# Half A's FFN in half B's order, four weight-sum jobs elsewhere, and the conditioning weights through the second merge

## The chip, the cores and the metric

One core of a Trainium2 chip runs the whole layer in one launch. The metric is device time in microseconds (us): the median of the runs, and beside it one execution with a hardware profile. The engines are named as in the profile: PE (TensorE), DVE (VectorE), ACT (ScalarE), POOL (GpSimd) and SP (SyncE, which here only issues DMAs).

## The reference

A layer for 1024 prompt tokens and 8 x 4 sample tokens, which share weights. The parts around the change:

```python
mod = silu(c) @ ada_w + ada_b                 # conditioning: shifts, scales, gates per sequence
sh1, sc1, gt1, sh2, sc2, gt2 = split(mod, 6)
u = (rmsnorm(x, g1) * (1 + sc1) + sh1) @ w_in # u_x, u_g, u_q, u_k, u_v, u_r, u_lr, u_ga, u_gb
h_lru = rg_lru(causal_conv(u_x)); y_a = h_lru * gelu(u_g)
y_b = rmsnorm(gla(u_q, u_k, u_v, ...)) * silu(u_r)
m = sigmoid(u_ga) * (y_a @ proj_a) + sigmoid(u_gb) * (y_b @ proj_b)
x = x + gt1 * (m @ w_out)
h2 = rmsnorm(x, g2) * (1 + sc2) + sh2
f1, f2 = split(h2 @ ffn_w1, 2)                # d_model 1024, d_ff 2816
x = x + gt2 * ((silu(f1) * f2) @ ffn_w2)
```

All is float32, and the last columns of `mod` (scale and gate of the FFN) are not needed before the second norm.

## The kernel before

**Halves.** The tokens are worked in two halves, one after the other: A has N = 512 prompt tokens, B has 544 (512 prompt tokens and the 32 sample tokens). Activations lie transposed, channels on partitions in tiles of 128 and tokens along the columns. D is 8 tiles, the FFN's inner width 22 tiles (f0 to f21), the recurrence's 10.

**Products.** Each float32 operand is split into a high and a low part of type fp32r; a product is three matmuls (lines L452, L453, L454). A weight comes by an SP DMA into a buffer of the pool "raw" (5 buffers, `load_raw`, L145), is split by ACT (L154, high part) and DVE (L155, the rest) into a buffer of the pool "hl" (3 buffers), and is used at the full width of 512 columns, or in A's output projection and first FFN tiles in two pieces of 256 columns.

**The fast form.** `products` (L1421, L1429 to L1431) computes a 2 x 2 block product with 7 block products in place of 8. It works on half the columns (256 in A), and needs sums of weight blocks and of activation blocks. Weight sums are made on the chip and kept in device memory: by `weight_sums` (tiles `s1<f>`, `s2<f>`: two SP loads of 512 KB into "raw", four DVE steps L352 to L355, two POOL stores L356 and L357 into `wsum<f>`; one job for each f, taken one at a time with `next(sums_of)`), and by `paced_sums` (the pool "sums", POOL loads L388, DVE L392 to L396, POOL stores L398). A tile f in the fast form is 84 matmuls for both weight halves; the second product of six k tiles in the fast form (`ffn2_fast`) is 252 in place of 144 of full width. For the latter, `keep` stores the block sums of the activations instead of the tiles.

**The FFN of A before.** `back`: after the output projection (`out_proj` on columns 0 to 255, then 256 to 511), f0 to f3 in two column pieces (`ffn1_first`), f4 and f5 whole (`ffn1`), f6 to f10 fast, then the second product over k tiles 0 to 10 directly (`ffn2(0, 11)`, out `f3psa`), with four sum jobs at its output tiles j = 0, 2, 4, 6; then f11 to f21 fast, and `ffn2(11, 22)`. B does f0 to f3, `ffn2(0, 4)`, f4 to f10 fast, `ffn2_fast(0)` over k tiles 4 to 9, and so on.

**Conditioning.** `ada_w` comes in 12 column chunks cc of four 512 KB loads (`ada<cc><k>`, L203, into an S buffer), each used by a group of small matmuls (`adaps<cc>`, L212; eight records in the profile), and closed by a transpose (`adat`, L223). `s.ada(1)` gives out one step. Chunks 0 to 9 are done earlier; what is left, cc 10 and 11 for the most part, was drained just before the merge of A. The merge (`merge_a`) has eight steps j: 24 matmuls for the gate (`gapsa<j>`), 30 for the projection (`papsa<j>`, weights `pa0a<j>` and `pa1a<j>`). Before it, `merge_b` does the same for the other branch (`pbpsa<j>`), with the last pair of recurrence tiles (`lma8`, `laa9`, `yaa8`, `yaa9`) between.

**What sets the order.** A tile scheduler orders the instructions of each engine by its own estimates and by the pools: S (17 large buffers), X (8), T (6). Each engine works its list strictly in order; SP's list is the order of the loads, and a load that waits for a buffer holds all behind it.

Of the kernel before, what the change touches and what calls it, by code (L numbers as in the profile page):

```python
# [27 lines left out]
LEVELS = (64, 32, 16, 8, 4, 2, 1)  # L28
EPS = 1e-6
EARLY = 4  # L30
FAST = (6, 4)
KF = (3, 2, 1, 0, 4, 6, 8, 5, 7, 9, 10, 12, 14, 11, 13, 15, 16, 17, 18, 19, 20, 21)
KORD = (0, 2, 4, 6, 1, 3, 5, 7)
GATES = KD // 2
# [20 lines left out]
def hybrid_layer(ctx, tc, I, O):  # L55
# [25 lines left out]
    tp = ctx.enter_context(tc.tile_pool(name="tp", bufs=6))  # L81
    axp = ctx.enter_context(tc.tile_pool(name="axp", bufs=2, space=PSUM))
    drp = ctx.enter_context(tc.tile_pool(name="drp", bufs=1, space=bass.MemoryType.DRAM))
    wsum = {f: drp.tile([P, 2048], F32, name=f"wsum{f}") for f in range(FAST[1], NF)}
    wsumg = [drp.tile([P, 2048], F32, name=f"wsumg{c}") for c in range(GATES)]
    wsum2 = {(q, g): drp.tile([P, 1536], F32, name=f"wsumf{q}{g}") for q in range(4) for g in range(2)}

# [259 lines left out]

    def weight_sums():

        for f in range(FAST[0], NF):  # L350
            r1, r2 = load_raw(I["ffn1"][2 * f], 1024, f"s1{f}"), load_raw(I["ffn1"][2 * f + 1], 1024, f"s2{f}")
            dve.tensor_add(r2[:, 512:1024], r2[:, 0:512], r2[:, 512:1024])  # L352
# [9 lines left out]
    def paced_sums():  # L362

        jobs = []
        halves = lambda t, u, c: t.rearrange("p (n u) -> p n u", n=2)[:, :, c * u:(c + 1) * u]
        def columns(sums, src):
            for c in range(2):
                to = [halves(sums[:, v * 1024:(v + 1) * 1024], 256, c) for v in range(2)]
                jobs.append((256, [halves(t, 256, c) for t in src], to))

        def rows(g):
            for q in range(4):
                c = P * (4 + 6 * g)
                to = [halves(wsum2[q, g][:, v * 768:(v + 1) * 768], 384, 0) for v in range(2)]
                jobs.append((384, [halves(I["ffn2"][2 * q + v][:, c:c + 768], 384, 0) for v in range(2)], to))

        for f in range(FAST[1], FAST[0]):
            columns(wsum[f], [I["ffn1"][2 * f + v] for v in range(2)])
        rows(0)
        for c in range(GATES):  # L380
            columns(wsumg[c], [I["w_in"][T_GA + 2 * c + v] for v in range(2)])
        rows(1)
        for k, (u, src, to) in enumerate(jobs):
            r = [wp.tile([P, 768], F32, tag="sums", name=f"sums{k}{v}", bufs=2) for v in range(2)]
            rv = [t[:, :2 * u].rearrange("p (n u) -> p n u", n=2) for t in r]
            for v in range(2):
                pool.tensor_copy(r[v][:, 0:1], pace[0][:, 0:1])
                pool.dma_start(rv[v], src[v])  # L388
            yield 1
            r1, r2 = rv  # L390
            last = len(traced())
            dve.tensor_add(r2[:, 1], r2[:, 0], r2[:, 1])  # L392
            behind(last)
            dve.tensor_sub(r2[:, 0], r1[:, 0], r2[:, 0])
            dve.tensor_sub(r1[:, 0], r2[:, 1], r1[:, 0])
            dve.tensor_sub(r1[:, 1], r1[:, 1], r1[:, 0])  # L396
            for v in range(2):
                pool.dma_start(to[v], rv[v])  # L398
            yield 1
# [3 lines left out]
    class Half:  # L403
        def __init__(s, hf):
            s.hf, s.N = hf, WID[hf]
            s.n = "ab"[hf]

            s.whole = (0, s.N, None, None)
            s.parts = [(0, 256, 0, 0), (256, 256, 0, 256)] if hf == 0 else [(0, 272, 0, 0), (272, 272, 1, 0)]
            s.tiled = None if hf == 0 else [(0, 256, 0, 0), (256, 288, 1, 0)]  # L410
            s.halves = s.parts if hf == 0 else [(o, w, 0, 0) for o, w, _, _ in s.parts]
            s.adas = ada_rest() if hf == 0 else iter(())
            s.early = {}
            s.lr_raw = None
# [673 lines left out]
        def lru_gate(s, nb, m, xc):  # L1088
            N, n = s.N, f"{s.n}{nb}"
            gw = load_raw(I["lru_w"][nb], 256, "lw" + n)  # L1090
            g1, g2 = s.wide("g1" + n), s.wide("g2" + n)
            for g, c in (g1, 0), (g2, P):
                for o, w, bank, off in [(0, HP, 0, 0)] if s.hf == 0 else s.parts:
                    pe.matmul(g[:, bank, off:off + w], gw[:, c:c + P], xc[:, o:o + w], start=True, stop=True)
            tr, ti = T("tr" + n), T("ti" + n)
            for t, g, b in (tr, g1, nb), (ti, g2, 10 + nb):
                for o, p in s.over(t, g):
                    act.activation(o, p, AF.Tanh, scale=0.5, bias=vh[:, b:b + 1])
            dve.scalar_tensor_tensor(ti[:, :N], ti[:, :N], 1.0, xc[:, :N], op0=OP.add, op1=OP.mult)
            if nb < NR - 1:  # L1100
                both = S("la" + n)
                a, hh = both[:, :N], both[:, 544:544 + N]
            else:
                a, hh = [xp.tile([P, 544], F32, tag="X", name=k + n)[:, :N] for k in ("la", "lh")]
            s4 = sp4[:, nb:nb + 1]
            act.activation(a[:, :N], tr[:, :N], AF.Exp, scale=s4, bias=s4)
            act.activation(tr[:, :N], tr[:, :N], AF.Tanh, scale=s4, bias=s4)
            act.activation(m, a[:, :N], AF.Square)
            dve.scalar_tensor_tensor(m, m, 1.0, tr[:, :N], op0=OP.add, op1=OP.mult)
            return a, hh, ti  # L1110
# [160 lines left out]
        def merge_a(s):  # L1271
            s.m = []
            for j in range(KD):
                tg = s.gate_a(j)
                s.join(j, tg, s.over(tg, s.branch_a(j)))
                s.keep_m(j)
                next(sums_late, None)
                if j % 3 < 2 and j < 7:
                    next(sums_of, None)
# [162 lines left out]
        def keep(s, f, tg):  # L1442

            N, W = s.N, s.N // 2
            if not (s.hf and 4 <= f < 16):
                a = s.act[f] = S(f"fa{s.n}{f}", F32R)
                split(a, tg[:, :N], N)
                return
# [23 lines left out]
        def ffn2_fast(s, g):  # L1472
# [43 lines left out]
        def ffn1_fast(s, fs):  # L1516
# [9 lines left out]
            for f in fs:  # L1526
                n = f"{s.n}{f}"
                pa, pb, pc = [mm(f"f{c}ps{n}")[:, 0, :W] for c in "abc"]
                v1, v2 = T("va" + n), T("vb" + n)
                tg = s.kept(f) if s.hf and f < 16 and f % 2 == 0 else T("ft" + n)  # L1530
                hi, lo, nn = slice(0, W), slice(W, N), slice(0, N)
                product(pa, "11", True)
                s.snap(v1[:, lo], pa)
# [30 lines left out]
        def ffn1(s, fs):
            for f in fs:
                a = s.act[f] = S(f"fa{s.n}{f}", F32R)
                yield from s.pair(f, s.whole, a)
# [34 lines left out]
        def finish(s, part, acc, queues=(pool,)):  # L1602
# [6 lines left out]
            for j in range(0, KD, 2):  # L1609
# [5 lines left out]
                    yield 0.0  # L1615
                (queues[j // 2 % len(queues)]).dma_start(out[:, j:j + 2, o:o + w], y2)

        def back(s):
            s.x, s.h2 = [], []
            p0, p1 = s.halves  # L1620
            a0, a1 = [ACC("20" + s.n)], [ACC("21" + s.n)]
            drain(s.out_proj(p0, a0))
            o1 = s.out_proj(p1, a1)
            next(o1)
            next(o1)
# [6 lines left out]
            mix(s.norm2(p1, a1), f)  # L1632
            drain(f)
            b = s.block_sums(s.h2)
            if s.hf == 0:
                mix(chain(s.ffn1_first(p1, EARLY), s.ffn1(range(EARLY, FAST[0]))), b)
                drain(b)
                drain(s.ffn1_fast(range(FAST[0], 11)))
                for j, _ in enumerate(s.ffn2(0, 11, s.whole)):
                    if j % 2 == 0:  # L1640
                        next(sums_of, None)
                return
            s.fs = {k: [] for k in ("11", "21", "22", "t1", "t2", "t3", "t4")}
            mix(chain(s.ffn1_first(p1, EARLY), s.ffn2(0, 4, s.whole)), b)
            drain(b)
            drain(s.ffn1_fast(range(4, 11)))
            drain(s.ffn2_fast(0))
            drain(s.ffn1_fast(range(11, 17)))
            drain(s.ffn2_fast(1))
            s.keep(16, s.late)  # L1650

        def branches(s, before):
# [19 lines left out]
                next(l, None)  # L1672
                s.ada(1)
            drain(l)
            drain(s.adas)
            if s.hf:
                pool.dma_start(O["tails"], tails)
            s.merge_a_fast() if s.hf else s.merge_a()
# [11 lines left out]
    derive()  # L1690
    A.branches(None)
    drain(sums_of)
    A.act = {}
    drain(A.ffn1_fast(range(11, NF)))
    acc = [ACC("3a")]
    dn = A.ffn2(11, NF, A.whole, acc)
    next(dn)
    B.load_x(pool)
    mix(chain(B.norm1_sum(), B.norm1()), dn)
# [117 lines left out]
```

## Time and profile before

| | |
|---|---|
| median of 3 runs | 1961.77 us (1960.86 to 1966.2) |
| profiled execution | 1960.34 us, span 1958.6 us |
| PE busy | 1926.0 us, 98% of the span |
| DVE, ACT, POOL busy | 69%, 50%, 7% |
| granted PE clock | 0.997 on the mean |
| matmuls | 13380 records |

The profile is of one execution. "Busy" of PE counts pipelined matmuls, so the time between the starts of two matmuls says more than their length. A wait is put down to the event that came last.

### The profile page before, as it was taken

The page shows a single profiled execution, that of the slowest core. Times are in us where ns is not written, and L with a number is a line of the kernel's source. Part 1 is how long each engine was busy: PE and PEld are TensorE (multiplying, and loading weights), DVE is VectorE, ACT ScalarE, POOL GpSimd, SP SyncE. Part 2 cuts the span into 40 slices and gives each one's busy share as a digit, 9 for nine tenths or more (in the row PEclk, how much of TensorE's full clock was granted, in tenths as well). Part 3 has the DMA queues.
Part 4 walks back from the last instruction along what each step waited for, and adds up shares of the span by engine and source line. Part 5 has one row for each costly group of instructions (what it writes and reads, how often), then busy time and mean ns, then how long its engine had stood idle before and what let it go on. Part 6 is the DMA issues. An engine that isn't in the chain of part 4 may idle for free. (4 is left out here: it accounts for less than half of the span.)

```text
span 1958.6 us, 33971 instructions
## 1 busy us (share of the span) xinstructions
PE 1926.0 (98%) x13380; PEld 1753.1 (90%) x13380; DVE 1360.2 (69%) x2420; ACT 973.2 (50%) x1559; POOL 140.7 (7%) x279
## 2 busy tenths in 40 slices
PE   9999999998999999999999999999999999999997
PEld 5877877776899998999899998999999999999997
DVE  5638487774658774677664497786467688888867
ACT  4645375542235552555353366675244354656653
POOL 0000001121100000000000001041201000000000
PEclk9999999999999999999999999999999999999999
DMA  8324235578764357554332413334446534555553
GB/s 341 108 97 165 73 108 193 195 264 315 260 235 157 128 179 247 189 183 156 119 119 68 145 49 96 128 115 148 145 140 226 199 130 131 177 170 179 178 163 104
DMA packets 122240, 319.24 MB, mean 163 GB/s; under 512 B 14560, under 2 KB 29664, under 8 KB 122080
## 3 DMA queue, kind: packets, MB, share of 16 engines
q1 hardware_dynamic: 107536, 263.89, 40.9%
q0 software_dynamic: 14000, 52.62, 7.4%
q8 instruction: 105, 1.72, 0.4%
q10 hardware_dynamic: 544, 0.56, 0.1%
q14 instruction: 55, 0.45, 0.1%
HBM read 278.42 MB, written 38.59 MB: 162 GB/s over the span
## 5 line engine op out<-in xcount | busy, mean ns | idle before, releaser
L155 DVE TENSOR_TENSOR fwa_hl<-fwa,fwa_hl 128x1024 fp32r<-128x1024 f32 (+1 forms) x57 | 68.8, 1207 | 44.6 <-ACT fwa_hl L154 43.6
L155 DVE TENSOR_TENSOR fwb_hl<-fwb,fwb_hl 128x1024 fp32r<-128x1024 f32 (+1 forms) x64 | 77.2, 1207 | 27.7 <-ACT fwb_hl L154 27.7
L154 ACT ACTIVATE fwa_hl<-fwa 128x1024 fp32r<-128x1024 f32 (+1 forms) x57 | 59.3, 1040 | 44.0 <-PE fapsa L1431 10.8
L154 ACT ACTIVATE fwb_hl<-fwb 128x1024 fp32r<-128x1024 f32 (+1 forms) x64 | 66.6, 1041 | 23.4 <-PE fcpsb L1431 9.0
L452 PE MATMUL f3psa<-faa,f3a_hl 128*128 128x512 f32 x176 | 68.6, 390 | 0.6 <-ACT f3a_hl L154 0.6
L454 PE MATMUL f3psa<-faa,f3a_hl 128*128 128x512 f32 x176 | 68.5, 390 | 0.4 <-DVE f3a_hl L155 0.4
L453 PE MATMUL f3psa<-faa,f3a_hl 128*128 128x512 f32 x176 | 68.6, 390 | 0.0
L154 ACT ACTIVATE f3a_hl<-f3a_raw 128x768 fp32r<-128x768 f32 (+1 forms) x32 | 25.4, 792 | 55.7 <-PE f3psa L454 47.4
L155 DVE TENSOR_TENSOR f3a_hl<-f3a_raw,f3a_hl 128x768 fp32r<-128x768 f32 (+1 forms) x32 | 28.3, 888 | 17.4 <-ACT f3a_hl L154 17.0
L452 PEld LDWEIGHTS f3psa<-faa,f3a_hl 128*128 128x128 f32 x176 | 33.0, 188 | 7.7 <-ACT f3a_hl L154 1.0
L454 PEld LDWEIGHTS f3psa<-faa,f3a_hl 128*128 128x128 f32 x176 | 33.0, 188 | 7.6 <-DVE f3a_hl L155 0.9
L453 PEld LDWEIGHTS f3psa<-faa,f3a_hl 128*128 128x128 f32 x176 | 33.0, 188 | 6.8
L352 DVE TENSOR_TENSOR s_raw<-s_raw 128x512 f32<-128x512 f32 x16 | 11.1, 691 | 37.9 <-DMA s_raw<-in_ffn 37.8
L454 PE MATMUL wopsb<-mb,wob_hl 128*128 128x272 f32 x128 | 36.9, 288 | 0.0
L452 PE MATMUL wopsb<-mb,wob_hl 128*128 128x272 f32 x128 | 36.9, 289 | 0.0
L453 PE MATMUL wopsb<-mb,wob_hl 128*128 128x272 f32 x128 | 36.8, 288 | 0.0
L453 PE MATMUL wopsa<-ma,woa_hl 128*128 128x256 f32 x128 | 36.4, 284 | 0.0
L454 PE MATMUL wopsa<-ma,woa_hl 128*128 128x256 f32 x128 | 36.2, 283 | 0.0
L452 PE MATMUL wopsa<-ma,woa_hl 128*128 128x256 f32 x128 | 36.1, 284 | 0.0
L212 PE MATMUL adaps<-ada,cth 128*32 128x256 f32 x384 | 29.5, 397 | 6.2 <-DMA ada<-in_ada_w 6.0
L452 PE MATMUL uxpsa<-h1a,uxpsa_hl 128*128 128x512 f32 x80 | 32.3, 403 | 0.0
L155 DVE TENSOR_TENSOR fvb_hl<-fvb,fvb_hl 128x768 fp32r<-128x768 f32 x28 | 26.8, 956 | 7.7 <-ACT fvb_hl L154 7.4
(2404 smaller groups left out, 7944.9 us busy)
## 6 DMA issues: line engine op xcount, KB each, us to landing
ada<-in_ada_w SPq DMA_DIRECT2D x48, 512.0 KB, 7.9
fwb<-wsum SPq DMA_DIRECT2D x72, 256.0 KB, 3.4
s_raw<-in_ffn SPq DMA_DIRECT2D x32, 512.0 KB, 4.3
wsum<-s_raw POOLq DMA_DIRECT2D x32, 512.0 KB, 4.2
fwa<-wsum SPq DMA_DIRECT2D x64, 256.0 KB, 3.3
fwb<-in_ffn SPq DMA_DIRECT2D x54, 256.0 KB, 3.4
fwa<-in_ffn SPq DMA_DIRECT2D x48, 256.0 KB, 3.1
woa_raw<-in_w_out SPq DMA_DIRECT2D x13, 512.0 KB, 4.2
```

The lines of the kernel that those rows point to most:

```text
L154: act.activation(hl[:, 0, :n], raw[:, :n], AF.Copy)
L155: dve.tensor_sub(hl[:, 1, :n], raw[:, :n], hl[:, 0, :n].bitcast(F32))
L212: pe.matmul(ps[32 * g:32 * g + 32, c:c + 256], cth[:, 4 * (k % 2) + g, :], raw[:, g * 256:(g + 1) * 256], start=(k % 2 == 0), stop=(k % 2 ...
L352: dve.tensor_add(r2[:, 512:1024], r2[:, 0:512], r2[:, 512:1024])
L452: pe.matmul(out, wh, x[:, o:o + w], start=st, stop=False)
L453: pe.matmul(out, wh, x[:, N + o:N + o + w], start=False, stop=False)
L454: pe.matmul(out, wl, x[:, o:o + w], start=False, stop=en)
```

## The change

- `BLOCKS` gives each half the end of its blocks: A keeps block sums of f4 to f9 (B, as before, of f4 to f15). A's FFN now runs f0 to f3, `ffn2(0, 4)`, f4 to f10 fast, `ffn2_fast(0)`, f11 to f21 fast, `ffn2(10, 22)`. `ffn1` is gone.
- The four sum jobs 18 to 21 go from `ffn2(0, 11)` to `out_proj` (j = 1, 4) and `ffn2(0, 4)` (j = 3, 6).
- `drain(s.adas)` before the merge is gone; the merge takes two conditioning steps in each j.
- The last exponential of A's recurrence (`laa9`) lies in an S buffer in place of X buffers.

```diff
-FAST = (6, 4)
+RAW0, BLOCKS = 6, (10, 16)
...
-            if nb < NR - 1:
+            if s.hf == 0 or nb < NR - 1:
                 both = S("la" + n)
...
                 tg = s.gate_a(j)
+                s.ada(1)
                 s.join(j, tg, s.over(tg, s.branch_a(j)))
                 s.keep_m(j)
+                s.ada(1)
...
-            if not (s.hf and 4 <= f < 16):
+            if not EARLY <= f < s.blocks:
                 a = s.act[f] = S(f"fa{s.n}{f}", F32R)
...
+        def raw_jobs(s, g, at):
+            for j, w in enumerate(g):
+                if s.hf == 0 and j in at:
+                    next(sums_of, None)
+                yield w
...
-            drain(s.out_proj(p0, a0))
+            drain(s.raw_jobs(s.out_proj(p0, a0), (1, 4)))
...
-            if s.hf == 0:
-                mix(chain(s.ffn1_first(p1, EARLY), s.ffn1(range(EARLY, FAST[0]))), b)
-                drain(b)
-                drain(s.ffn1_fast(range(FAST[0], 11)))
-                for j, _ in enumerate(s.ffn2(0, 11, s.whole)):
-                    if j % 2 == 0:
-                        next(sums_of, None)
-                return
             s.fs = {k: [] for k in ("11", "21", "22", "t1", "t2", "t3", "t4")}
-            mix(chain(s.ffn1_first(p1, EARLY), s.ffn2(0, 4, s.whole)), b)
+            mix(chain(s.ffn1_first(p1, EARLY), s.raw_jobs(s.ffn2(0, 4, s.whole), (3, 6))), b)
             drain(b)
             drain(s.ffn1_fast(range(4, 11)))
             drain(s.ffn2_fast(0))
+            if s.hf == 0:
+                return
...
             drain(l)
-            drain(s.adas)
...
-    dn = A.ffn2(11, NF, A.whole, acc)
+    dn = A.ffn2(10, NF, A.whole, acc)
```

**SP at the start of the merge**, before: the loads from the sum job 12 on (`ada100` is the first load of chunk 10, `gapsa0` the gate's weight of step 0, `s113` and `s213` a sum job's).

```order
L145 DMA s212_raw_3666<-in_ffn1 128x1024
L203 DMA ada100_3345<-in_ada_w 128x1024
L145 DMA gapsa0_raw_3742<-in_w_in 128x1024
L145 DMA pa0a0_raw_3774<-in_proj_a 128x640
L145 DMA pa1a0_raw_3794<-in_proj_a 128x640
L145 DMA s113_raw_3825<-in_ffn1 128x1024
L145 DMA s213_raw_3827<-in_ffn1 128x1024
L145 DMA gapsa1_raw_3836<-in_w_in 128x1024
L203 DMA ada101_3566<-in_ada_w 128x1024
L203 DMA ada102_3626<-in_ada_w 128x1024
```

And now, from the load of `pa1a0` on:

```order
L145 DMA pa1a0_raw_3750<-in_proj_a 128x640
L145 DMA s113_raw_3781<-in_ffn1 128x1024
L145 DMA s213_raw_3783<-in_ffn1 128x1024
L145 DMA gapsa1_raw_3792<-in_w_in 128x1024
L203 DMA ada100_3344<-in_ada_w 128x1024
L145 DMA pa0a1_raw_3834<-in_proj_a 128x640
L145 DMA pa1a1_raw_3854<-in_proj_a 128x640
L145 DMA s114_raw_3892<-in_ffn1 128x1024
L203 DMA ada101_3565<-in_ada_w 128x1024
L203 DMA ada102_3625<-in_ada_w 128x1024
```

`ada100` moved from ahead of `gapsa0` to behind `gapsa1`, and `ada101` from there to behind `s114`; `ada103` and `ada110` follow it, `ada111` and `ada112` stand now behind the sum job 15.

**SP in merge step 3**, now (before, no conditioning load stood here):

```order
L145 DMA pa1a4_raw_4159<-in_proj_a 128x640
L145 DMA s116_raw_4190<-in_ffn1 128x1024
L145 DMA s216_raw_4192<-in_ffn1 128x1024
L203 DMA ada113_3986<-in_ada_w 128x1024
L145 DMA gapsa5_raw_4201<-in_w_in 128x1024
```

The last conditioning load came into this stretch, behind the sum job 16.

**PE around the end of `pbpsa7`**, before, with the second group of chunk 10 (`adaps10` from `ada101`):

```order
L452 MATMUL pbpsa7_3632<-yba7_2243,pba7_hl_3635 128x512
L212 MATMUL adaps10_3565<-ada101_3566,cth_141 32x256 x4
L453 MATMUL pbpsa7_3632<-yba7_2243,pba7_hl_3635 128x512
L454 MATMUL pbpsa7_3632<-yba7_2243,pba7_hl_3635 128x512
L452 MATMUL gapsa0_3741<-h1a0_333,gapsa0_hl_3744 128x512
```

And now, with the first (from `ada100`):

```order
L452 MATMUL pbpsa7_3631<-yba7_2243,pba7_hl_3634 128x512
L212 MATMUL adaps10_3564<-ada100_3344,cth_141 32x256 x4
L453 MATMUL pbpsa7_3631<-yba7_2243,pba7_hl_3634 128x512
L454 MATMUL pbpsa7_3631<-yba7_2243,pba7_hl_3634 128x512
L452 MATMUL gapsa0_3691<-h1a0_333,gapsa0_hl_3694 128x512
```

In the same place stands now the group before it; the second, third and fourth stand in `papsa0`, behind 11, 16 and 21 of its matmuls.

More of the change, by code (lines that the diff above doesn't have):

```diff
@@ L83, in hybrid_layer @@
     drp = ctx.enter_context(tc.tile_pool(name="drp", bufs=1, space=bass.MemoryType.DRAM))
-    wsum = {f: drp.tile([P, 2048], F32, name=f"wsum{f}") for f in range(FAST[1], NF)}
+    wsum = {f: drp.tile([P, 2048], F32, name=f"wsum{f}") for f in range(EARLY, NF)}
     wsumg = [drp.tile([P, 2048], F32, name=f"wsumg{c}") for c in range(GATES)]
@@ L348, in weight_sums @@
     def weight_sums():
-        for f in range(FAST[0], NF):
+        for f in range(RAW0, NF):
             r1, r2 = load_raw(I["ffn1"][2 * f], 1024, f"s1{f}"), load_raw(I["ffn1"][2 * f + 1], 1024, f"s2{f}")
@@ L375, in rows @@
                 jobs.append((384, [halves(I["ffn2"][2 * q + v][:, c:c + 768], 384, 0) for v in range(2)], to))
-        for f in range(FAST[1], FAST[0]):
+        for f in range(EARLY, RAW0):
             columns(wsum[f], [I["ffn1"][2 * f + v] for v in range(2)])
@@ L405, in __init__ @@
             s.hf, s.N = hf, WID[hf]
-            s.n = "ab"[hf]
+            s.n, s.blocks = "ab"[hf], BLOCKS[hf]
             s.whole = (0, s.N, None, None)
@@ L1529, in ffn1_fast @@
                 v1, v2 = T("va" + n), T("vb" + n)
-                tg = s.kept(f) if s.hf and f < 16 and f % 2 == 0 else T("ft" + n)
+                tg = s.kept(f) if f < s.blocks and f % 2 == 0 else T("ft" + n)
                 hi, lo, nn = slice(0, W), slice(W, N), slice(0, N)
@@ L1562, in ffn1_first @@
                 yield from s.pair(f, part, s.act[f])
[L1564 to L1567, printed above, removed]
         def ffn2(s, k0, k1, part, acc=None):
@@ L1647, in back @@
             drain(s.ffn2_fast(0))
+            if s.hf == 0:
+                return
             drain(s.ffn1_fast(range(11, 17)))
@@ L1692, in hybrid_layer @@
     drain(sums_of)
-    A.act = {}
     drain(A.ffn1_fast(range(11, NF)))
     acc = [ACC("3a")]
-    dn = A.ffn2(11, NF, A.whole, acc)
+    dn = A.ffn2(10, NF, A.whole, acc)
     next(dn)
```

## The prediction

> **What bounds the kernel now.** I read the page first, then busy time by stage, then the tensor engine (PE) and the load queue (SP) where a stage loses time.
>
> ```profile
> span 1958.6 us, 33971 instructions
> ...
> PE 1926.0 (98%) x13380; PEld 1753.1 (90%) x13380; DVE 1360.2 (69%) x2420; ACT 973.2 (50%) x1559; POOL 140.7 (7%) x279
> ```
>
> PE is the bound. A change gains only by fewer or shorter matmuls, or by taking away a PE wait; work for VectorE (DVE) and DMAs costs only where PE runs out of cover. The stages, by windows (columns: busy time and count of each engine, granted clock, DMA share, GB/s):
>
> ```profile
> core 0: us, PE busy (x) PEld busy (x) DVE busy (x) ACT busy (x) POOL busy (x), PEclk, DMA share, GB/s
> 437.40:475.20 37.80, 32.22 (x174) 21.57 (x175) 18.15 (x36) 8.07 (x12) 5.42 (x10) 0.91 0.89 320
> 475.20:561.10 85.90, 85.90 (x379) 70.87 (x378) 48.23 (x67) 25.95 (x35) 14.09 (x29) 1.00 0.76 265
> 561.10:608.60 47.50, 47.50 (x394) 47.12 (x393) 34.32 (x66) 21.89 (x34) 1.09 (x2) 1.00 0.57 193
> ...
> 658.60:680.30 21.70, 21.70 (x97) 17.98 (x97) 13.21 (x22) 7.85 (x13) 0.00 (x0) 1.00 0.48 145
> 680.30:730.60 50.30, 50.30 (x421) 50.26 (x421) 36.82 (x54) 29.09 (x48) 0.54 (x1) 1.00 0.51 160
> 730.60:790.50 59.90, 59.90 (x266) 49.59 (x265) 30.47 (x41) 14.16 (x18) 3.73 (x7) 1.00 0.72 249
> ...
> 1662.00:1734.00 72.00, 72.00 (x577) 72.00 (x577) 58.08 (x91) 43.05 (x73) 0.00 (x0) 1.00 0.52 162
> 1734.00:1764.00 30.00, 30.00 (x243) 30.00 (x242) 24.52 (x48) 18.62 (x33) 0.00 (x0) 1.00 0.61 195
> ```
>
> In order: the start of half A's merge, its seven later steps, the output projection, FFN tiles 4 and 5 whole, tiles 6 to 10 in the fast form, the second product over k tiles 0 to 10 (with four sum jobs); then half B's fast tiles and its second product in blocks. All but the first are full. In the first PE idles 5.6 us and the clock falls:
>
> ```profile
> 448.31 0.39 PE L452 MATMUL pbpsa<-yba,pba_hl 128*128 128x512 f32 x1
> 454.28 1.08 PE L212 MATMUL adaps<-ada,cth 128*32 128x256 f32 x8 [5.58 <-DMA ada<-in_ada_w]
> 455.30 0.80 PE L453 MATMUL pbpsa<-yba,pba_hl 128*128 128x512 f32 x1
> ...
> 460.37 0.50 PE L453 MATMUL gapsa<-h1a,gapsa_hl 128*128 128x512 f32 x1
> ```
> ```profile
> 441.00:448.70 7.70, 7.70 (x34) 6.03 (x33) 1.87 (x3) 2.84 (x4) 0.56 (x1) 1.00 0.99 337
> 448.70:451.80 3.10, 0.00 (x0) 0.00 (x0) 0.07 (x1) 0.00 (x0) 0.00 (x0) 1.00 0.93 344
> 451.80:458.70 6.90, 4.42 (x21) 1.95 (x22) 6.87 (x13) 0.74 (x1) 2.54 (x4) 0.51 1.03 415
> ```
>
> PE waits for one conditioning weight (ada101) with the DMA engines full, and after 3.1 us of idling runs at half clock until 458.7: 4.42 us of work at 0.51, so some 2.2 us more are lost. A shorter idle elsewhere left the clock alone (the windows row around it shows 1.00):
>
> ```profile
> 1177.00:1181.00 4.00, 1.63 (x13) 1.32 (x13) 4.00 (x9) 1.44 (x4) 0.00 (x0) 1.00 0.50 142
> ```
>
> [...]
>
> **The change part by part.**
>
> *FFN of half A.* Tiles 4 and 5 were 96 matmuls of 512 columns in 21.7 us. In the fast form five tiles (420 matmuls of 256 columns) took 50.3 us, 119.8 ns each and 10.06 us a tile; two cost 20.1. Gain 1.6 us. In the second product six k tiles (6 x 8 x 3 = 144 matmuls at 59.9/264 = 226.9 ns, 32.7 us) become 252 half-width ones at 119.8 ns, 30.2 us. Gain 2.5 us. Together 4.1, if A's blocks keep that pitch. PE's weight loads are as busy as PE at half width (50.26 of 50.30), so this pitch leaves nothing over; the block product breaks even at 32.7/252 = 129.6 ns. Both ends: B's 272-column blocks run at 30.0/242 = 124 ns, which would leave 1.4 us of the 2.5; and nothing in the trace goes below 119.8. I take 119.8, A's own width. The added keeping of block sums is DVE work; B, which keeps them already, has DVE busy 58.1 of 72.0 us and PE without a gap, so I cost it at nothing; A's 256-column steps are some 3% shorter, and if that cover went, DVE's excess would come straight onto PE.
>
> [...] The rows above have 226.9 and 119.8 at these very widths, and the measurement decides; I give it 1 in 100.
>
> *Conditioning.* In the row order ada100 loses its early place: it was loaded at 429.0, and now stands in the queue behind gapsa1's load, where ada101 stood:
>
> ```profile
> 429.02 0.33 SPq L203 DMA_DIRECT2D ada<-in_ada_w  x1
> 436.60 0.33 SPq L145 DMA_DIRECT2D gapsa_raw<-in_w_in  x1
> ...
> 444.27 1.24 SPq L145 DMA_DIRECT2D s_raw<-in_ffn  x2
> 445.60 0.38 SPq L145 DMA_DIRECT2D gapsa_raw<-in_w_in  x1
> 446.03 9.72 SPq L203 DMA_DIRECT2D ada<-in_ada_w  x7
> ```
>
> It waits there for a buffer that PE frees in pbpsa7, and PE asks for it two matmuls before pbpsa7's end, exactly where it stood idle. So I expect the stall to stay and only change its name. How long it takes to land is shown by the loads issued from 446.03, from 444.2, from 485.9, from 502.6 and from 453.4 (three lines):
>
> ```profile
> ada<-in_ada_w SPq DMA_DIRECT2D x1, 512.0 KB, 8.2
> ...
> s_raw<-in_ffn SPq DMA_DIRECT2D x2, 512.0 KB, 6.3
> ...
> s_raw<-in_ffn SPq DMA_DIRECT2D x2, 512.0 KB, 3.2
> ...
> s_raw<-in_ffn SPq DMA_DIRECT2D x2, 512.0 KB, 6.3
> ...
> wsum<-s_raw POOLq DMA_DIRECT2D x2, 512.0 KB, 8.0
> ada<-in_ada_w SPq DMA_DIRECT2D x1, 512.0 KB, 10.5
> ```
>
> One 512 KB load less stands ahead of it (524 KB at 415 GB/s: 1.3 us), and PE comes some 0.7 us earlier, since one group of conditioning matmuls has left the stretch before. The stall is then 5.6 - 1.3 + 0.7 = 5.0 us if the queue is full throughout, 5.6 if not. I take 5.2: gain 0.4, with the clock's 2.2 as before. Ends: 3.2 us to landing in place of 8.2 would leave 0.2 of it, 10.5 makes it 7.5.
>
> The other seven loads and their groups go into merge steps 0 to 3, which have no idle time now. A group is the same work wherever it stands, so that adds nothing; a late load does. ada101 now stands behind s114's load, which waits for the second store of the sum job before it: the job's data lands at about 450.5, four DVE steps of 0.7 us, a store of 4 to 8 us, 457 to 461; two transfers of 1.3 us later it is there, 460 to 464. PE, resumed at 453.2, has 37 matmuls to do (10 at half clock, 27 at 0.227), and comes at about 464. Wait 0 to 2; I take 0.5. ada102 and 103 follow 1.3 us apart, and PE has 5 matmuls and a group between them (1.8 us): nothing. In merge step 2, ada111 stands right behind the second load of a sum job: about in time, 0 to 1.5; 0.5. ada113 is the tight one. It stands behind s216, which waits for pa1a3's split; of step 2's end at 499.7 this split ended 1.9 us later:
>
> ```profile
> 500.72 0.83 DVE L155 TENSOR_TENSOR pa1a_hl<-pa1a_raw,pa1a_hl 128x640 fp32r<-128x640 f32 x1
> ```
>
> PE needs it 24 + 3 matmuls and a group after step 2's end, 6.8 us; 4.4 us are left from issue, for a load that takes 3.2 to 6.3 us at this place, plus 1.3 behind s216. Wait 0 to 3.2; I take 1.5. Together +2.5.
>
> *la9 in the large pool.* Its exponential now waits for a buffer that PE frees in pbpsa7, so the recurrence's last pair moves on DVE behind the sum job s213. Data at about 450.5, four steps of 0.7, then some fifteen of 0.4 to 1.2: ready at about 465; PE needs yaa8 last in papsa0, at about 469. Hidden by 4 us; were the ada stall gone, by 1 or less.
>
> *Four sum jobs.* Each is two loads on SP, two stores on POOL and four DVE steps:
>
> ```profile
> L352 DVE TENSOR_TENSOR s_raw<-s_raw 128x512 f32<-128x512 f32 x16 | 11.1, 691 | 37.9 <-DMA s_raw<-in_ffn 37.8
> ...
> wsum<-s_raw POOLq DMA_DIRECT2D x7, 512.0 KB, 3.8
> ```
>
> Two move into the output projection (DVE 34.3 of 47.5 us; 8 x 0.69 = 5.5 more). Behind them stand woa03, which waits for a store, and on DVE woa00's split. A store of 3.8 to 8 us puts woa03's split at 565 to 569, needed at 569.6. Two move into the second product over k tiles 0 to 3 (96 matmuls, 21.8 us); there the fast form's second weight pair waits for a store, with 2 us to spare at 3.8 us a store and 2 too few at 8. Cost 0 to 3; I take 0.7. They leave the long second product, which had no gap: no gain.
>
> **Sum.** The profiled execution took 1960.3 us (span 1958.6 and 1.7 around it), 1.4 under the median of the runs, 1961.8. 1960.3 - 1.6 - 2.5 - 0.4 + 2.5 + 0.7 = 1959.0; half a microsecond for the median's place gives 1959.5.
>
> **Rivals.** *(a) The stall goes.* If ada100 lands in 3 to 4 us, PE waits under 1 us, and the clock stays up: 5.2 - 0.8 + 2.2 = 6.6 less, 1952.9; with no late ada load afterwards, 1950.4. For it: seven ada loads no longer crowd the queue. Against: those stood behind ada101, and what stood ahead (s113, s213, gapsa1, two stores) is still there. 0.15.
>
> *(b) The merge stays short of data: slower than before.* Place: adaps10's second group in papsa0. If ada100 and ada101 take the 10.5 us of the row above, ada100 costs 2.3 more, and ada101, issued at about 458 to 459, lands at 469 while PE comes at 466: 3 us, then at 3.1 us of idling another half-clock stretch of 2.2, and ada113 waits 6 in place of 1.5: 1959.5 + 2.3 + 2.5 + 2.2 + 4.5 = 1971. It decides from a second wait of over 3.1 us. For it: DMA share 0.99 and 1.03 in the two stretches. Against: the loads are spread over 50 us. 0.16.
>
> *(c) A's blocks lose their gain* (pitch at 129.6 ns, or a wait of 2.5 us for a pool buffer, since 18 activation tiles now ask for 17): 1962. B's even run speaks against. 0.09.
>
> **Chances.** The forecast 0.59, with its own range 1955.5 to 1964; the rivals as given. 0.3% of the time, 5.9 us, is about what a measurement tells from no change: under 1955.9 is faster, over 1967.7 slower. Faster: (a) and 0.04 of the forecast's low end, 0.19. [...] The range reaches into (a) and (b): 1951.5 to 1968.
>
> **What would show it.** PE's wait for ada of 5 us at about 448 and clock 0.5 behind it: the stall stays; both absent: (a). PE waits for ada near 464 and 505: the late loads, (b) if over 3 us. The fast tiles 4 and 5 at 10.06 us each and A's block product at 30.2 us: the FFN's gain; longer, (c). I would be wrong above all by a load that lands earlier or later than its neighbours did before.

## The result: 0.7% slower, and the profile after

The changed kernel took 1976.0 us (median of 6 runs, 1973.3 to 1984.4) against 1962.1 for the kernel before (6 runs, 1959.1 to 1966.2): 1.0072 times as long, 95% interval 1.0050 to 1.0095. The forecast, 1959.5 with a range of 1951.5 to 1968, was wrong. The profiled execution took 1975.9 us. Its page:

```profile
span 1974.1 us, 34508 instructions
...
PE 1930.1 (98%) x13560; PEld 1765.1 (89%) x13560; DVE 1388.7 (70%) x2475; ACT 992.1 (50%) x1602; POOL 147.3 (7%) x279
```

PE is busy only 4.1 us longer than before, while the span grew by 15.5: most of the loss is idle time. By windows (columns as in the prediction; the merge is counted from the last gate of the branch before it, the last `gbpsa` group, and every other stage from its first matmul), the kernel before:

```profile
431.66:561.12 129.46, 123.86 (x579) 96.88 (x578) 70.46 (x108) 35.47 (x49) 21.77 (x42) 0.97 0.79 280
561.12:608.60 47.48, 47.48 (x394) 47.12 (x393) 34.32 (x66) 21.89 (x34) 1.09 (x2) 1.00 0.57 193
608.60:964.95 356.35, 353.56 (x2382) 327.23 (x2381) 250.26 (x420) 172.09 (x274) 6.39 (x12) 1.00 0.53 173
964.95:1958.57 993.62, 975.01 (x7789) 956.15 (x7787) 718.53 (x1375) 509.98 (x872) 79.47 (x153) 1.00 0.43 140
```

and after:

```profile
432.00:566.14 134.14, 125.17 (x580) 97.97 (x578) 76.67 (x117) 40.93 (x55) 27.94 (x44) 0.97 0.78 275
566.14:619.64 53.50, 49.33 (x394) 48.65 (x392) 34.10 (x63) 19.98 (x30) 2.17 (x4) 0.97 0.70 240
619.64:978.88 359.24, 352.28 (x2562) 334.51 (x2561) 275.50 (x474) 193.28 (x321) 4.25 (x8) 1.00 0.54 171
978.88:1974.15 995.27, 976.24 (x7789) 957.60 (x7787) 718.70 (x1375) 510.01 (x872) 79.55 (x153) 0.99 0.44 139
```

In order: A's merge (+4.7 us), its output projection (+6.0), its FFN (+2.9), and all of B with the end (+1.6). With 0.3 ahead of the merge that is the 15.5. The output projection, full before, now has 4.2 us without a matmul and a lower clock (0.97 in place of 1.00). PE's waits after, by the timeline (in brackets the idle time before, and what ended it):

```profile
449.12 0.64 PE L212 MATMUL adaps<-ada,cth 128*32 128x256 f32 x8 [0.97 <-DMA ada<-in_ada_w]
...
459.48 0.64 PE L212 MATMUL adaps<-ada,cth 128*32 128x256 f32 x8 [1.11 <-DMA ada<-in_ada_w]
...
463.77 0.50 PE L454 MATMUL papsa<-yaa,pa1a_hl 128*128 128x512 f32 x1 [1.28 <-DVE pa1a_hl L155]
...
489.36 0.64 PE L212 MATMUL adaps<-ada,cth 128*32 128x256 f32 x8 [1.94 <-DMA ada<-in_ada_w]
...
506.95 1.08 PE L212 MATMUL adaps<-ada,cth 128*32 128x256 f32 x8 [3.67 <-DMA ada<-in_ada_w]
...
588.75 0.39 PE L454 MATMUL wopsa<-ma,woa_hl 128*128 128x256 f32 x1 [1.23 <-DVE woa_hl L155]
...
600.28 0.58 PE L459 MATMUL nps2a<-ones,acc20a 128*128 128x1 f32 x4 [2.51 <-DVE acc20a L487]
...
700.03 0.38 PE L1431 MATMUL fapsa<-t12a,fwa_hl 128*128 128x256 f32 x1 [3.92 <-ACT vaa L1439]
```

The 5.58 us stall at the start of the merge is gone (0.97). Seven others of over 1 us took its place, and around those of 3.67, 2.51 and 3.92 us PE ran at half clock (0.50 from 506.4 to 513.3, 602.0 to 605.4, 701.0 to 704.4).

**The output projection.** Two sum jobs stand here now. What is short is the residual input `xra`, by the grouped waits from 566 to 620 us (columns: us in total, times, longest), the load queue's own waits and SP's list:

```profile
DVE xma L1330 <- DMA xra<-in_xa: 8.9, 5, 3.7
```
```profile
SPq L145 <- DMA wsum<-s_raw: 4.3, 2, 3.6
```
```profile
580.63 1.47 SPq L1338 DMA_DIRECT2D xra<-in_xa  x1
586.12 0.33 SPq L145 DMA_DIRECT2D woa_raw<-in_w_out  x1
586.50 0.62 SPq L1338 DMA_DIRECT2D xra<-in_xa  x1
```

The weight's load needs the "raw" buffer that the job holds until a store of it has landed (issued at 579.58, landed 6.5 us later at 586.06). From 582.1 to 586.1 SP issues nothing, and the small `xra` loads behind, which need no such buffer, are late with it. DVE waits for them, so the sum of squares `acc20a` is late, and PE idles 2.5 us at the end of the stage. The longest of DVE's waits, 3.7 us, is not of this kind: its load was issued at 580.63, ahead of the hold, and took 6.4 us to land. Behind the step that waited for it, at 587.48, stands a weight's split on DVE, and PE waits 1.23 us for that split (588.75).

A first delay came earlier. DVE stood idle for 3.05 us, until 573.01, at a job's first step, whose load had not landed. The split of a weight stood behind it (574.48), and SP's next load behind that split (from 569.3 to 575.7).

**The boundary to tile f4.** The other two jobs stand just ahead of it. ACT's list there:

```profile
696.04 1.06 ACT L154 ACTIVATE fwa_hl<-fwa 128x1024 fp32r<-128x1024 f32 x1 [4.59 <-DMA fwa<-wsum]
698.65 1.06 ACT L154 ACTIVATE fwa_hl<-fwa 128x1024 fp32r<-128x1024 f32 x1 [1.55 <-DMA fwa<-in_ffn]
699.62 0.37 ACT L1439 ACTIVATE vaa<-fapsa 128x256 f32<-128x256 f32 x1
```

`vaa` takes a product out of PSUM, and PE waits for it. It needs neither of the two weights split ahead of it, but in ACT's list it stands behind both, and they came late (two of these loads were issued at 690.6 and 690.9, just after the second store of a job landed at 690.5). Not all of the 3.92 us is `vaa`'s: PE's wait began at 696.1, and the product that it was to start needs the first of the two weights, whose part on ACT ended at 697.1. So about 1 us would have been lost without `vaa` (an estimate from these rows).

### The profile page after: what moved, and what is told of

Same layout as the page of the kernel before. It is cut to its first block, busy times and chain, and to the rows that moved or that the text cites. A ratio compares the mean times of both kernels' runs of the same rounds, so it can differ in the third digit from the quotient of the medians.

```text
span 1974.1 us, 34508 instructions
## 1 busy us (share of the span) xinstructions
PE 1930.1 (98%) x13560; PEld 1765.1 (89%) x13560; DVE 1388.7 (70%) x2475; ACT 992.1 (50%) x1602; POOL 147.3 (7%) x279
## 5 line engine op out<-in xcount | busy, mean ns | idle before, releaser
L155 DVE TENSOR_TENSOR fwa_hl<-fwa,fwa_hl 128x1024 fp32r<-128x1024 f32 (+1 forms) x64 | 77.3, 1208 | 40.3 <-ACT fwa_hl L154 40.2
L154 ACT ACTIVATE fwa_hl<-fwa 128x1024 fp32r<-128x1024 f32 (+1 forms) x64 | 66.6, 1040 | 36.5 <-PE fapsa L1433 12.3
L452 PE MATMUL f3psa<-faa,f3a_hl 128*128 128x512 f32 x128 | 50.0, 392 | 0.9 <-ACT f3a_hl L154 0.9
L453 PE MATMUL f3psa<-faa,f3a_hl 128*128 128x512 f32 x128 | 49.9, 390 | 0.0
L454 PE MATMUL f3psa<-faa,f3a_hl 128*128 128x512 f32 x128 | 49.6, 389 | 0.0
L154 ACT ACTIVATE f3a_hl<-f3a_raw 128x768 fp32r<-128x768 f32 (+1 forms) x24 | 18.5, 773 | 33.5 <-PE f3psa L454 17.8
L452 PE MATMUL uxpsa<-h1a,uxpsa_hl 128*128 128x512 f32 x80 | 32.3, 403 | 0.0
L212 PEld LDWEIGHTS adaps<-ada,cth 128*32 128x32 f32 x384 | 10.0, 113 | 23.8 <-issue 12.7
L453 PE MATMUL uxpsa<-h1a,uxpsa_hl 128*128 128x512 f32 x80 | 31.2, 390 | 0.0
L454 PE MATMUL uxpsa<-h1a,uxpsa_hl 128*128 128x512 f32 x80 | 31.2, 390 | 0.0
```

Source lines behind the costliest of these rows:

```text
L154: act.activation(hl[:, 0, :n], raw[:, :n], AF.Copy)
L155: dve.tensor_sub(hl[:, 1, :n], raw[:, :n], hl[:, 0, :n].bitcast(F32))
L212: pe.matmul(ps[32 * g:32 * g + 32, c:c + 256], cth[:, 4 * (k % 2) + g, :], raw[:, g * 256:(g + 1) * 256], start=(k % 2 == 0), stop=(k % 2 ...
L452: pe.matmul(out, wh, x[:, o:o + w], start=st, stop=False)
L453: pe.matmul(out, wh, x[:, N + o:N + o + w], start=False, stop=False)
L454: pe.matmul(out, wl, x[:, o:o + w], start=False, stop=en)
```

## The experiments

Stage lengths are of the one profiled execution of each kernel, ratios of all its runs. A's FFN is given in three pieces: f0 to f3; then up to f11 (the second product over k tiles 0 to 3, f4 to f10 and the product in blocks; their matmuls alone take 122.6); then the rest.

| kernel | merge | output projection | A's FFN | f0-f3, to f11, rest | B, end | ratio to before, 95% interval |
|---|---|---|---|---|---|---|
| before | 129.5 | 47.5 | 356.4 | other order | 993.6 | 1 |
| after | 134.1 | 53.5 | 359.2 | 51.5, 128.3, 179.5 | 995.3 | 1.0072 (1.0050 to 1.0095) |
| merge_old_jobs_fast | 129.2 | 47.5 | 354.4 | 49.4, 125.5, 179.5 | 998.2 | 1.0004 (0.9992 to 1.0016) |
| jobs_fast | 135.7 | 47.5 | 360.6 | 49.6, 131.5, 179.5 | 995.2 | 1.0049 (1.0030 to 1.0068) |
| ada_drained | 132.9 | 52.4 | 360.1 | | 1000.4 | 1.0080 (1.0057 to 1.0103) |
| ada_only | 134.8 | 47.5 | 356.5 | other order | 996.7 | 1.0045 (1.0028 to 1.0061) |
| la9_only | 129.8 | 47.5 | 356.7 | other order | 993.5 | 1.0014 (1.0004 to 1.0023) |
| ada_two_ahead | 128.4 | 52.2 | 360.5 | | 1000.2 | 1.0079 (1.0064 to 1.0094) |
| ffn_jobs_merge | 150.3 | 47.9 | 351.3 | 49.2, 122.6, 179.5 | 997.1 | 1.0087 (1.0062 to 1.0113) |
| ffn_jobs_ada | 142.9 | 47.5 | 352.1 | | 996.3 | 1.0070 (1.0045 to 1.0095) |
| ffn_jobs_late | 129.3 | 47.5 | 362.6 | 50.0, 122.6, 190.0 | 993.1 | 1.0033 (1.0023 to 1.0044) |
| ada_spread | 124.1 | 47.5 | 356.1 | other order | 998.5 | 0.9984 (0.9973 to 0.9995) |
| ffn_ada | 126.5 | 47.5 | 363.2 | 51.4, 122.6, 189.2 | 1000.2 | 1.0007 (0.9995 to 1.0020) |
| ada_spread_ffn | 126.5 | 47.5 | 357.0 | 50.1, 127.4, 179.5 | 993.6 | 0.9996 (0.9984 to 1.0007) |

B's matmuls are the same number in all rows; its column moves by 7 us with the clock, on which the last section says more. The stages of A are therefore the better witness.

### The parts one by one

**jobs_fast**: after, with the four jobs in the fast tiles f4 to f10.

```diff
-            drain(s.raw_jobs(s.out_proj(p0, a0), (1, 4)))
+            drain(s.out_proj(p0, a0))
...
-s.raw_jobs(s.ffn2(0, 4, s.whole), (3, 6))
+s.ffn2(0, 4, s.whole)
...
-            drain(s.ffn1_fast(range(4, 11)))
+            drain(s.raw_jobs(s.ffn1_fast(range(4, 11)), (1, 4, 7, 10)))
```

> The changed kernel with only the four sum jobs moved, from the output projection (j 1, 4) and the second product over k tiles 0 to 3 (j 3, 6) into half A's fast tiles f4 to f10. Ledger theory (the jobs cause the 6.0 us lost in the output projection and the 5.3 us at f4): 1976 - 11.3 = 1965. Rival (the output projection loses its 6 us because the merge comes late and its weights and xra loads with it): only the wait at f4 goes, 1971.

```profile
567.48:614.95 47.48, 47.48 (x393) 47.11 (x392) 34.32 (x65) 21.88 (x34) 1.09 (x2) 1.00 0.58 193
```

Without jobs the output projection is back at 47.48 us with no gap, to the hundredth what it was before. Its 6.0 us are the two jobs' doing: shown. The FFN gained nothing, since the jobs hurt among the fast tiles too (131.5 in place of 122.6 up to f11, with 6.8 us at half clock from 726.2). The total, 1971.7, is about the rival's 1971, but the rival's reason is refuted: the merge was as late here (135.7 us), and the output projection lost nothing.

**ada_drained**: after, with the conditioning steps drained before the merge again.

```diff
-                s.ada(1)
                 s.join(j, tg, s.over(tg, s.branch_a(j)))
                 s.keep_m(j)
-                s.ada(1)
...
+            drain(s.adas)
```

> The changed kernel with the conditioning drained before the merge again (la9 stays in the S pool, jobs stay moved). Ledger theory: the waits for ada111 and ada113 and the half clock after them go (some 8 us), the first stall stays short or comes back by up to 5 us: 1970 to 1974, with the output projection still 53 us. Rival (output projection late because of the conditioning): 1964 to 1968.

The merge shortened by 1.2 us only, to 132.9: the late waits for `ada` went, 4.0 us of waits for `ada` came back, and the wait for `pa1a_hl` grew from 1.28 to 3.5 us. The total did not fall: 1978.6, where 1970 to 1974 was expected.

**ada_only**: the reverse of that edit on the kernel before, and nothing else.

> The kernel before with only the conditioning moved: no drain before the merge, two steps in each merge step j. Ledger theory: PE waits for ada in the merge steps as in the changed kernel (2 to 4 us each, one with the clock at half), the first stall goes: +3 to +6, 1965 to 1968, output projection unchanged at 47.5 us. Rival (the waits come of ada100's late place, which la9 causes, not of the spreading): the first stall of 5.6 us goes and no other comes, 1953 to 1956.

PE's waits in its merge, grouped (us in total, times, longest):

```profile
PE adaps L212 <- DMA ada<-in_ada_w: 8.7, 2, 4.7
```

The move alone makes the merge 5.3 us longer. Here the first stall stays (4.05 us), and the wait for `ada113` (4.65) with a half-clock stretch from 505.9 to 512.7 (0.50) is new. So the late load is the move's price, and the move alone does not take the first stall away: `ada100` kept its early place here (issued at 429.55).

**la9_only**: before, with the last exponential in an S buffer.

```diff
-            if nb < NR - 1:
+            if s.hf == 0 or nb < NR - 1:
```

> The kernel before with one change: la9, the last exponential of half A's recurrence, in an S buffer in place of X buffers. With it ada100's load falls behind gapsa1's in the queue and the recurrence's last pair behind a sum job on DVE. If la9 alone makes the merge dearer (as the run with the conditioning drained suggests, 132.9 us from the last gate to the output projection against 129.5): merge +2 to +4, a wait for ada100 of 1 to 4 us and one of papsa0's weights of 2 to 4 us behind it, 1964 to 1966. Rival (the moved jobs or the spread conditioning did that): merge as before, 1962.

```profile
PE adaps L212 <- DMA ada<-in_ada_w: 3.7, 2, 2.0
PE papsa L454 <- DVE pa1a_hl L155: 2.7, 1, 2.7
```

With this edit alone `ada100` is issued at 444.18 in place of 429.02, so its new place is `la9`'s doing and not that of the spread conditioning. The first stall falls to 2.0, and a wait for `pa1a_hl` appears that the kernel before does not have: an exchange, the merge as long as before, as the rival expected. The total is 0.04 to 0.23% longer.

**merge_old_jobs_fast**: the changed FFN with the merge of before (the edits of ada_drained and jobs_fast, and `la9` back).

> The changed kernel with its merge put back as it was (conditioning drained before the merge, la9 in X buffers) and with the four sum jobs put into half A's fast tiles f4 to f10 (two steps apart) in place of the output projection and the second product; only the FFN order of the change is left. Ledger theory (the loss of the changed kernel is three separate stalls: merge +5.0, output projection +6.0, boundary before f4 +5.3, and the FFN itself gains 4): 4 us under before, 1958, merge and output projection as in before (37.8 and 47.5 us for those windows), no wait at f4. Rival (the new order is itself short of DVE, whose block sums crowd the stretch before f4): a wait of 3 to 5 us at f4 stays without the jobs, 1962 to 1966.

The merge is 129.2 and the FFN 354.4: 2.0 less than before, of the 4 to 5 that the FFN alone gains (next). In this profile B, with three half-clock steps of 3.41 us that the profile of before does not have, takes it back; the times are equal, where 4 us less was expected.

### What the four jobs cost, wherever they stand

**ffn_jobs_merge**: as the last, but with the jobs in the merge, one taken in every step of its two loops.

```diff
-                if j % 3 < 2 and j < 7:
-                    next(sums_of, None)
+                next(sums_of, None)
...
-                if s.hf == 0 and j:
+                if s.hf == 0:
                     next(sums_of, None)
```

> The new FFN order of half A with the merge's conditioning and la9 as in the kernel before, and all sixteen sum jobs done in the two merges, one in each step (before: seven and five, and four in the second product), where weights of full width give each job 5.4 us of PE work a weight. Theory (the FFN order itself gains 4 us and jobs cost nothing under full-width weights): no wait in output projection, at f4 or in f4 to f10, 1958. Rival (the queue of the merge has no room, DMA share 0.76 there): waits of 2 to 6 us in the merge, 1960 to 1964.

This kernel and ffn_jobs_ada (below) have no job in the FFN of A, so they give the FFN's price (first row: up to f11):

```profile
679.08:801.69 122.61, 122.61 (x939) 118.60 (x938) 95.81 (x153) 70.04 (x119) 0.00 (x0) 1.00 0.59 179
...
801.69:981.20 179.51, 178.61 (x1235) 166.85 (x1233) 127.00 (x207) 95.13 (x148) 2.14 (x4) 1.00 0.53 167
```

Not one gap up to f11, and 351.3 us in all: 5.0 less than before (352.1 in ffn_jobs_ada, 4.3 less). The part that was changed, from f4's old place on, takes 302.1 against 306.4 before, 4.3 less; the other 0.8 here lies in f0 to f3. But the merge pays 21 us for the jobs (four waits for `gapsa_hl`, 15.1 us in all, with four half-clock stretches, from 513.9, 534.4, 551.5 and 568.6).

**ffn_jobs_late**: the jobs in the fast tiles f11 to f16.

```diff
-    drain(sums_of)
-    drain(A.ffn1_fast(range(11, NF)))
+    drain(A.raw_jobs(A.ffn1_fast(range(11, NF)), (1, 4, 7, 10)))
+    drain(sums_of)
```

> The new FFN order of half A with merge, conditioning and la9 as in the kernel before, and the four sum jobs in the fast tiles f11 to f16 of half A, where no block sums are kept and DVE is busy 71%. Theory (a job stalls fast tiles only where DVE is crowded): output projection 47.5, no wait at f4 and at most 1 us in the fast tiles, half A's FFN 4 to 5 us under before's 356.4, time 1957. Rival (a job stalls any stretch of half-width weights, since two of the five weight buffers are held until the store lands): four waits of about 1 us, no gain, 1961 to 1963.

```profile
781.54:971.58 190.04, 181.35 (x1235) 168.58 (x1234) 135.46 (x224) 95.20 (x149) 6.39 (x12) 0.99 0.63 202
```

10.5 us longer than without jobs (179.51), in waits for `vaa`, `vba` and `fwa_hl` (3.1, 2.3 and 2.4 us). No block sums are kept here and DVE is busy 135.5 of 190.0 us, 71%, so the loss does not need a DVE crowded by them; that theory fell, and the time, 1966.5, lies above the rival's too. What fits is the buffers: a job holds two of the five "raw" buffers from its loads until its stores have landed. No run here had more of them, so this is argued and not shown.

So four jobs cost 13.9 us where the change put them (6.0 in the output projection, 359.2 - 351.3 = 7.9 in the FFN; 7.1 against ffn_jobs_ada's FFN, and then 13.2 together), 2.9 to 8.9 in f4 to f10, 9.7 to 10.5 in f11 to f16, and 21 in the merge. Of the 7.9, 5.6 lie between f3 and f11 and 2.3 in f0 to f3, where no job stands: the three kernels with jobs in the output projection take 51.5 to 52.1 there, the others 49.2 to 50.1 (51.4 in ffn_ada, with a half-clock step). The jobs cost nothing in one place that was seen: beside the long second product of full width, which the change took away (before, from 730.60 to 790.50, PE busy 59.90 of 59.90 us).

### Mending the merge

**ada_two_ahead**: after, with each conditioning load from `ada102` on issued two groups ahead in place of one.

```diff
-            if n < 48:
-                ada_next.append(ada_load(n // 4, n % 4))
+            for n in (n, n + 1) if n == 41 else (n + (n > 41),):
+                if n < 48:
+                    ada_next.append(ada_load(n // 4, n % 4))
```

> The changed kernel with the conditioning weights loaded two steps ahead in place of one, from chunk 10 on. Theory (ada111 and ada113 come late because they are asked for one step ahead, behind a sum job's loads): both waits (2.1 and 3.8 us) and the half clock behind the second (3) go, 1976 - 9 = 1967. Rival (the DMA engines are full in the merge, so an earlier place only makes other loads late): the waits go over to gapsa's or papsa's weights, 1973 to 1978.

```profile
431.69:560.05 128.36, 123.99 (x580) 97.23 (x579) 76.33 (x116) 40.85 (x55) 27.64 (x44) 0.99 0.79 285
```

The waits for `ada111` and `ada113` (1.94 and 3.67 us) are gone and the merge is 5.8 us shorter, though the first stall is back at 3.1: these were late loads, and an earlier issue cured them. The total stays at 1.0079: the two places of the jobs are as in the changed kernel, and in its profile B has four half-clock steps in place of one.

**ada_spread**: before, with conditioning through the merge, loads two ahead, and steps given out in the first 13 turns of `merge_b` only, so that the start of the merge is not crowded.

```diff
-            for w in s.merge_b():
+            for i, w in enumerate(s.merge_b()):
...
-                s.ada(1)
+                if i < 13:
+                    s.ada(1)
```

> The kernel before with the conditioning through the second merge, but the last two steps of the first merge give out none, and loads are asked for two ahead from chunk 10 on (FFN, jobs and la9 as before). Theory (the waits in the merge are loads asked for too late, the first stall a group asked for too early): the stall of 5.6 us and its half clock go, no wait over 1 us in the merge, which takes 122 to 123 us from the last gate on in place of 129.5: 1954. Rival (full queue): waits of 2 to 4 us stay, 1960 to 1966.

```profile
432.21:556.34 124.13, 122.35 (x580) 95.97 (x578) 70.05 (x109) 35.10 (x49) 23.47 (x42) 1.00 0.81 293
```

The merge takes 124.1 us, 5.3 less than before, at full clock, with waits of 1.7 us in all. Over ten runs the kernel is 0.16% faster than before (0.9984, 0.9973 to 0.9995): the one version that beats both. The median, 1957.5, is short of the 1954 expected. The margin is small, it was found among twelve versions, and ada_spread_ffn below, with the same edits of the merge and the new FFN, does not repeat it.

**ffn_jobs_ada, ffn_ada, ada_spread_ffn**: the new FFN with this conditioning and `la9` back, with the jobs in the merge (steps stop after 14 turns), in f11 to f16, and in f4 to f10.

> As the run before it in this call (new FFN order, sixteen sum jobs in the merges, la9 in X), with the conditioning through the second merge, but with ada101's step left out of the last step of the first merge and loads two ahead from chunk 10 on. Theory (the first stall is one of place: a group asked for 5 us too early, in a full queue): the stall of 5.6 us and its half clock (2.2) go and no wait over 1 us comes in the merge: 1950 to 1953. Rival (queue full: the load is late wherever it stands): waits of 2 to 4 us in steps 0 to 3, 1958 to 1964.

> Both of the runs before it in this call: new FFN order with the jobs in f11 to f16, conditioning spread as there, la9 in X. If their gains add up: 7 from the merge and 4 to 5 from the FFN, 1950; if the jobs still stall the fast tiles, 1953 to 1955.

> The conditioning as in the run ada_spread (two steps held back in the first merge, loads two ahead, la9 in X) with the new FFN order and the sum jobs in f4 to f10 as in merge_old_jobs_fast. If stages add up: merge 124 (5.3 less than before), output projection 47.5, half A's FFN 354.4 (2.0 less), so 7 under before, 1954, and faster than ada_spread alone by 2. Rival (a better merge moves the FFN's loads and jobs against each other): the FFN's 2 us go again, 1957 to 1958, as ada_spread.

The gains do not add up. The jobs bring their price with them (merge 142.9; f11 on 189.2; up to f11 127.4), and none of the three is measurably faster than before: the theories had 1950 to 1955, and the medians are 1974.1, 1963.7 and 1961.4.

## Why the prediction was wrong, step by step

- **The four jobs: the step that failed.** "Cost 0 to 3; I take 0.7" measured 13.9 (13.2 by ffn_jobs_ada). The prediction named both right places and what waits there: "Behind them stand woa03, which waits for a store", and the fast form's weights with "2 us to spare". It then timed only the named weights, and these cost little: PE waited 0.43 us for the split of `woa03` (575.75), and about 1 us of the 3.92 was the fast form's weight. It did not follow the lists behind them: the `xra` loads behind a weight's load on SP, a later weight's split behind `xma` on DVE, and on ACT the `vaa` behind two late splits. It also did not price the half clock that followed two of these gaps (one step of 3.41 us at 0.50 behind the 2.51 and one behind the 3.92, so up to 1.7 us each, an estimate from these figures).
- **The FFN: right.** -4.1 predicted; -5.0 and -4.3 measured in the two kernels without jobs in it, -4.3 in both for the part that was changed. Up to f11 the pitches of the prediction give 96 x 0.2269 + 840 x 0.1198 = 122.4; measured 122.61. Rival (c) fell, and so did the 1 in 100 that the prediction gave to a slower FFN, for which no run shows a ground: these 936 matmuls kept the trace's own pitch.
- **The first stall: wrong, for the better.** "I expect the stall to stay and only change its name", 5.2; it fell to 0.97. The load of `ada100` landed in 4.4 us after its issue at 444.55; the row that it was measured against, issued at 446.03, took 8.2:

```profile
ada<-in_ada_w SPq DMA_DIRECT2D x1, 512.0 KB, 4.4
```

  The queue had moved forward: the gate's weight was issued at 430.05 and not at 436.60. Before, it was held by a sum job's store, issued at 428.56 and landed 8.0 us later at 436.59; now that store was issued at 426.78 and landed 3.3 us later at 430.04. The prediction counted one load less on the way, 1.3 us, and not that wait for a buffer. The part of the change that decides is `la9`: in the five kernels that have it in an S buffer the gate's weight was issued at 428.9 to 432.4 and the stall was 0.97 to 3.26 us (2.0 in la9_only, which changes nothing else); in the five that have it in X buffers and the conditioning of the first merge as before, 436.0 to 437.1 and 4.05 to 5.58. Why the store lands sooner stays open.
- **Rival (a), the stall goes: half right.** The stall went, and the clock fell elsewhere.
- **The late conditioning loads: right place, wrong size.** `ada113` "wait 0 to 3.2; I take 1.5" measured 3.67 and a half-clock stretch (load landed 7.6 us after issue, not 3.2 to 6.3). `ada111`, "0 to 1.5", took 1.94, and `ada101`, "0 to 2; I take 0.5", 1.11. This is one part of rival (b), which gave `ada113` 6 us; at the place that it held decisive, the second group in `papsa0`, the wait was the 1.11. The merge cost +4.7 where the sum had +2.1.
- **la9: wrong.** The recurrence was ready when predicted (`yaa` at 464.9, "about 465"), and PE did not wait for it. But the split of the weight `pa1a` stands now behind its steps `tia`, `laa` and `gga` on DVE, and these behind a `sums` step that waited 4.82 us for its load:

```profile
457.18 0.42 DVE L392 TENSOR_TENSOR sums<-sums 128x256 f32<-128x256 f32 x1 [4.82 <-DMA sums<-in_ffn]
...
461.58 1.40 DVE L1138 SCALAR_TENSOR_TENSOR gga<-laa,gga 128x256 f32<-128x256 f32 x4
462.90 0.82 DVE L155 TENSOR_TENSOR pa1a_hl<-pa1a_raw,pa1a_hl 128x640 fp32r<-128x640 f32 x1
```

  "Hidden by 4 us" was said of the moved work itself; the work behind it had no such cover, and PE waited 1.28 us (2.7 in la9_only).

The size of the miss in one line: predicted -4.1 (FFN), +0.7 (jobs), +2.1 (merge), together -1.3; measured -5.0, +13.9, +4.7, +1.6 (B, with one half-clock step) and +0.3 (ahead of the merge), together +15.5.

## What to carry to other kernels

When work that holds buffers is moved, its price can be, as here (13.9 us for four jobs), not its own busy time or the one load that waits for it, but all that stands behind that load on each in-order list, down to the small transfer (`xra`, and 2.51 us of PE's time) or PSUM copy (`vaa`, most of 3.92 us) that has nothing to do with it. Before a change removes a stage in which such work was free, look for where else it would be free: here the FFN's 4 to 5 us could be had only by paying 3 to 21 for the four jobs. And the time that a load took to land is no property of its place in the list: in the same place `ada101` took 8.2 us before and `ada100` 4.4 after.

## What the hardware showed that was not expected

The clock did not answer to the length of a gap alone, as the prediction had it (3.1 us). In each of the thirteen profiles other than that of ffn_jobs_ada all its changes lie on one grid of 3.413 us: after, the falls at 14.91, 506.43, 602.01, 700.99 and 1598.70 us are 144, 28, 29 and 263 such steps apart. What counts, in these profiles, is how little PE does between two grid points. After, four steps of the grid, each with the step behind it where that ran at half clock:

```profile
485.95:489.36 3.41, 1.48 (x7) 0.90 (x5) 1.32 (x3) 1.54 (x2) 0.20 (x1) 1.00 1.02 384
...
503.02:506.43 3.41, 0.25 (x2) 0.00 (x0) 0.68 (x1) 1.20 (x2) 0.00 (x0) 1.00 0.81 332
506.43:509.84 3.41, 2.89 (x13) 1.70 (x14) 3.23 (x5) 0.60 (x1) 1.09 (x2) 0.50 0.37 153
...
598.59:602.01 3.42, 1.73 (x15) 1.76 (x16) 2.56 (x8) 1.32 (x2) 0.00 (x0) 1.00 0.34 96
602.01:605.42 3.41, 3.41 (x19) 3.41 (x18) 2.45 (x8) 1.67 (x3) 0.00 (x0) 0.50 0.49 157
...
697.58:700.99 3.41, 0.95 (x8) 0.96 (x9) 2.67 (x3) 2.34 (x4) 0.00 (x0) 1.00 0.99 373
700.99:704.41 3.42, 3.42 (x19) 3.42 (x18) 1.23 (x1) 0.60 (x2) 0.00 (x0) 0.50 0.96 349
```

In these thirteen profiles, past 400 us, every full-clock step with PE busy under 1.4 us was followed by half clock, and between 1.4 and 2.1 us some were (1.73 above) and some weren't (1.48 above). Above 2.1 us it happened only at one place in B, in six profiles, with 2.7 us busy, 78.5 us behind the place shown below; that is not explained. So the same gap cost nothing or a half-clock step by where it fell on the grid: at one place in B (`g1b1l`) PE idles 2.4 us in each of the thirteen; a half-clock step follows in seven, and none in six. That place, in the kernel before and in ada_spread:

```profile
1178.84:1182.26 3.42, 2.13 (x10) 1.85 (x11) 3.42 (x10) 1.34 (x3) 0.02 (x1) 1.00 0.52 158
1182.26:1185.67 3.41, 3.41 (x30) 3.41 (x29) 2.17 (x5) 3.38 (x7) 1.45 (x2) 1.00 0.39 154
```
```profile
1173.12:1176.53 3.41, 1.43 (x6) 1.25 (x7) 3.41 (x9) 0.83 (x3) 0.00 (x0) 1.00 0.51 156
1176.53:1179.94 3.41, 3.41 (x14) 3.10 (x13) 2.86 (x7) 3.38 (x7) 1.47 (x2) 0.50 0.26 68
```

Such falls are what moves B between 993 and 1000 us. With no half-clock step ahead of its end these profiles have 993.1 to 993.6 us for B, with one 995.2 and 995.3, with two 996.7 to 997.1, with three 998.2 to 998.5 and with four 1000.2 to 1000.4. That much of the spread between runs of one kernel comes from them too is likely, and not shown.

So a gap well under the 3.1 us of the prediction was enough: 2.51 us at 600.28 in the changed kernel, and the 2.4 us at `g1b1l` in seven profiles.
